# Every fourth plain residue, while wide pieces run, is summed by an accumulating DMA in place of VectorE

## The chip, the cores and the metric

The kernel runs on one core of a Trainium2 chip. The metric is the device time of one execution in microseconds (us), the median of several. TensorE's matmuls, VectorE, ScalarE and GpSimd each work through a queue of their own in the order in which the program was written; SyncE's queue issues the loads. In the rows they are PE (PEld for the loading of weights), DVE, ACT, POOL and SP.

## The reference

A trunk of two layers over 256 tokens of width 2048, all in float32. Layer 0 mixes by two groups of attention heads, layer 1 by latent attention, and each layer ends in a SwiGLU:

```python
for layer in range(DEPTH):
    ...
    x = layer_norm(DEEPNORM_ALPHA * x + y, ln_g[layer, 0], ln_b[layer, 0])
    y = swiglu(x, ffn_w_gate[layer], ffn_w_up[layer], ffn_w_down[layer])
    x = layer_norm(DEEPNORM_ALPHA * x + y, ln_g[layer, 1], ln_b[layer, 1])

def swiglu(x, w_gate, w_up, w_down):
    return (jax.nn.silu(x @ w_gate) * (x @ w_up)) @ w_down
```

w_gate and w_up are 2048 x 5632, w_down is 5632 x 2048. The change touches the two SwiGLU parts alone.

## The kernel before

**Split products.** A float32 product is made of three matmuls in TensorE's rounded float32 format. A weight w is split into a high part, w rounded, and a low part, the residue w - high; the activations lie split in the same way in XH and XL (or YH and YL). The sum is XH x high + XH x low + XL x high (`mm3`, L117 to L119). The low part is used by every second of the three matmuls, L118.

**Pieces.** All weights arrive in pieces of 256 rows. A *plain* piece is two times 512 columns (a tile of 128 x 1024): it is loaded from HBM into a raw tile by SyncE (L360), ScalarE rounds it into `wh` (L425), VectorE subtracts and writes the residue into `wl` (L427), and TensorE uses both in 12 matmuls of 512 columns, a *visit*. While a SwiGLU runs, other weights, most of w_gate and a part of w_up, go another way, which trades additions for matmuls (Strassen's scheme): these are the *wide* pieces. Their raw tile `sraw` gets sums of its own quarters from VectorE (L383 to L386), ScalarE rounds 128 x 1792 into `sh` (L389), VectorE writes the residue `sl` (L392), and TensorE uses them in 21 matmuls of 256 columns (L453 to L455). When the eighth wide piece of a chunk is done, VectorE combines four sums from PSUM, the *drain* (L483 to L489), and makes the product of gate and up (L1089, L1093); TensorE then transposes the result (L602).

**Order.** `visits` is the list of all visits, written out when the program is made; wide visits are strewn among plain ones at a rate that grows from 0.575 to 0.9 for one plain visit. `pieces` is the order in which pieces are first used. The feed keeps ahead of TensorE: after each visit that is a piece's last, its weight buffer is put back, and `feed_more` splits the next pieces (`feed_split`) for which a buffer is free, and issues loads (`feed_dma`) for which a raw tile is free. There are four raw tiles and four pairs `wh`, `wl` for plain pieces, two `sraw` and two pairs `sh`, `sl` for wide ones; while wide pieces run, the plain pieces keep to their four, which go round in turn. A wide piece's L389 and L392 are not issued with its sums but *owed*: a later split pays them (`pay`), each behind its own instruction on the same engine, and `feed_more` pays all that are older than one visit. A raw tile goes back to the list as soon as its residue has been issued; SyncE's next load into it waits on the chip until that residue is written.

`first_s` and `last_s` hold, for each layer, the positions in `pieces` of its first and last wide piece. GpSimd has small tasks in the layer norms (L978, L1006, L1007) and nothing between them in a SwiGLU.

Of the kernel before, what the change touches and what calls it, by code (L numbers as in the profile page):

```python
# [9 lines left out]
F32 = mybir.dt.float32  # L10
F32R = mybir.dt.float32r
AF = mybir.ActivationFunctionType
ALU = mybir.AluOpType
# [40 lines left out]
def trunk_kernel(ctx: ExitStack, tc: tile.TileContext, x, ab_w_in, b_f, ab_w_out,  # L54
                 rel_bias, mla_w_in, q_g, kv_g, w_uq, w_ukv, mla_w_out, w_gate, w_up,
                 w_down, ln_g, ln_b, cst, out):
    nc = tc.nc
# [67 lines left out]
    def add_chunk(name, xs, kslots, srcs, tags=None):  # L125
        subs = []
        o = 0
        for n in srcs[0]:
            subs.append((n, o))
            o += n  # L130
        c = Chunk(name, xs, kslots, subs, srcs[1], tags or ("mm",) * len(subs))
        c.n = o
        chunks[name] = c
        return c
# [28 lines left out]
    def rows(w, k0, cols):  # L163
        return [(o, n, w[k0:k0 + 256, c0:c0 + n].rearrange("(k p) c -> p k c", p=P))
                for o, n, c0 in cols]
# [3 lines left out]
    for g in range(4):  # L169
        q0, k0, v0 = ((QA, KA, VA) if g < 2 else (QB, KB, VB))  # L170
        h4 = HB4[g] % 8
        if g == 0:
            c = add_chunk("v0", "X", K16, ([260, 260], lambda h: rows(
                w0, h * 256, [(0, 520, VA + 512)])), ("mm", "att"))
        else:
            c = add_chunk(f"v{g}", "X", K16, ([512], lambda h, a=v0 + h4 * P: rows(
                w0, h * 256, [(0, 512, a)])))
        kmajor(c)
        for u in range(2):
            a = (h4 + 2 * u) * P  # L180
            c = add_chunk(f"qk{g}{u}", "X", K16, ([512], lambda h, a=a, q0=q0, k0=k0: rows(
                w0, h * 256, [(0, 256, q0 + a), (256, 256, k0 + a)])))
# [93 lines left out]
    c = add_chunk("m0", "X", K16, ([512], lambda h: rows(wi, h * 256, [(0, 512, 0)])))  # L276
    lead_begin(c)
    for i in (1, 2):
        c = add_chunk(f"m{i}", "X", K16, ([288], lambda h, i=i: rows(
            wi, h * 256, [(0, 288, 512 + 288 * (i - 1))])), ("att",) if i == 1 else None)  # L280
# [4 lines left out]
    for nm in order:  # L285
        p = int(nm[2:])
        if nm[0] == "u":
            c = add_chunk(nm, "X", [0, 1, 2, 3], ([384], lambda h, p=p: rows(
                w_uq[0], h * 256, [(0, 384, p * 384)])))
        else:  # L290
            c = add_chunk(nm, "X", [4, 5, 6, 7], ([512], lambda h, p=p: rows(
                w_ukv[0], h * 256, [(0, 512, p * 512)])))
# [6 lines left out]
    pieces = []  # L299
# [9 lines left out]
    first_s, last_s = {}, {}  # L309
# [4 lines left out]
    raw_free = [("N", feed.tile([P, HPMAX], F32, name=f"raw{i}")) for i in range(NR)]  # L314
# [5 lines left out]
    slot_of, rslot_of = {}, {}  # L320
# [20 lines left out]
    def take(free, j):  # L341
        ok = classes(j)
        for i, (k, t) in enumerate(free):
            if k in ok:
                return free.pop(i)
        return None
# [18 lines left out]
    whole = {}  # L365
    owed = []

    def pay(step):

        for o in list(owed):  # L370
            while o["fns"] and (step == "all" or o["age"] >= 1 and step == o["fns"][0][0]):
                o["fns"].pop(0)[1]()
            if not o["fns"]:
                owed.remove(o)

    def owe(key, act, dve, age=0):
        owed.append({"key": key, "age": age, "at": cur[0], "fns": [("act", act), ("dve", dve)]})

    def split_s(j):
        r = raws.pop(j)  # L380
        sh, sl = slot_of[j][1]
        v = r.rearrange("p (q c) -> p q c", c=256)
        nc.vector.tensor_tensor(v[:, 4:6], v[:, 0:1].broadcast_to([P, 2, 256]), v[:, 1:3],  # L383
                                op=ALU.subtract)
        nc.vector.tensor_tensor(v[:, 6], v[:, 1], v[:, 5], op=ALU.subtract)
        nc.vector.tensor_tensor(v[:, 7], v[:, 3], v[:, 6], op=ALU.subtract)  # L386

        def hi():
            nc.scalar.activation(sh, r[:, 256:2048], AF.Copy)  # L389

        def lo():
            nc.vector.tensor_tensor(sl, r[:, 256:2048], sh.bitcast(F32), op=ALU.subtract)  # L392
            raw_free.append(rslot_of.pop(j))
        wts[j] = (sh.rearrange("p (q c) -> p q c", c=256), sl.rearrange("p (q c) -> p q c", c=256))
        return hi, lo

    def feed_split(j, halves=False, part=None):
        if j >= len(pieces):
            return False
        c, h = pieces[j]  # L400
        n = 2 * c.n
        if part != 1:
            got = take(w_free, j) if j in raws else None
            if got is None:
                return False
            slot_of[j] = got
            if c.S:
                new = split_s(j)
                for o in owed:
                    o["age"] += 1  # L410
                pay("act")
                pay("dve")
                owe(j, *new)
                return True
            r = raws.pop(j)
            wh, wl = got[1]
            wts[j] = (wh[:, :n].rearrange("p (k c) -> p k c", k=2),
                      wl[:, :n].rearrange("p (k c) -> p k c", k=2))
            whole[j] = (r, wh, wl)
        r, wh, wl = whole[j]  # L420
        cuts = [(0, c.n), (c.n, n)] if halves or part is not None else [(0, n)]
        if part is not None:
            cuts = [cuts[part]]
        for a, b in cuts:
            nc.scalar.activation(wh[:, a:b], r[:, a:b], AF.Copy)  # L425
            pay("act")
            nc.vector.tensor_tensor(wl[:, a:b], r[:, a:b], wh[:, a:b].bitcast(F32),  # L427
                                    op=ALU.subtract)
            pay("dve")
        if part != 0:  # L430
            whole.pop(j)
            raw_free.append(rslot_of.pop(j))
        for o in owed:
            o["age"] += 1
        return True
# [7 lines left out]
    def feed_more(lim):  # L443
        fetch()
        while fs["nsp"] < min(lim, len(pieces)) and feed_split(fs["nsp"]):
            fs["nsp"] += 1
            fetch()
        if any(cur[0] - o["at"] >= 1 for o in owed):
            pay("all")
# [577 lines left out]
    def setup_ln(c3, nxt, final=False):  # L1027
# [20 lines left out]
        def split_a():  # L1048
            assert fs["nsp"] == p0 + 4
            assert feed_split(p0 + 4, part=0)  # L1050
            fs["nsp"] += 1
# [5 lines left out]
        at((c3.name, b0 + LEAD - 3, (1,)), lambda: (ln_T(0, 0), split_a(), ln_blk_act(0, 2)))  # L1057
        at((c3.name, b0 + LEAD - 2, (1,)), lambda: ln_T(0, 1))
        at((nxt.name, 1, (0,)), lambda: (ln_T(0, 2), feed_split(p0 + 4, part=1)))
        at((nxt.name, LEAD - 3, (0,)), lambda: (ln_T(1, 0), ln_blk(1, 1)))  # L1060
        at((nxt.name, LEAD - 2, (0,)), lambda: (ln_blk_act(0, 3), ln_blk(1, 2)))
# [295 lines left out]
    for i, (c, h, toks, *half) in enumerate(visits):  # L1357
# [21 lines left out]
        if last_use[c.name, h] == i:  # L1379
            j = pid[c.name, h]  # L1380
# [81 lines left out]
```

## Time and profile before

| | us |
|---|---|
| median of 3 runs | 2145.41 (2145.27 to 2146.47) |
| the profiled execution | 2146.55 |
| its span, first to last instruction | 2144.7 |
| TensorE busy | 2120.4 (99%) |
| VectorE busy | 1674.0 (78%) |
| ScalarE busy | 1061.6 (50%) |
| GpSimd busy | 94.5 (4%) |

The SwiGLU of layer 0 takes some 440 to 1140 us of the span and that of layer 1 the time from 1437 on; wide pieces run from 465 to 1050 and from 1455 to 2047. The granted clock of TensorE is 1.00 in nearly all of the span (mean 0.998), the higher of its two levels. A busy TensorE is not TensorE at its peak, since its matmuls overlap; what counts is whether it waits. In the rows "idle before <- releaser" is the time in which an engine had nothing to do ahead of an instruction, and what ended it.

### The profile page before, as it was taken

The numbers are of one execution on the slowest core, as the hardware profiler recorded it, in microseconds if no ns is written. First come the engines' busy times: TensorE is split into PE (matmuls) and PEld (weight loads), VectorE is DVE, ScalarE is ACT, GpSimd is POOL, SyncE is SP. The second block draws the span as 40 slices with busy tenths as digits, with TensorE's granted clock in tenths as the row PEclk, the third lists the DMA queues.
The fourth block names the chain that finished last, engine by engine and source line by source line (L and its number), as shares of the span: only waits on it lengthen the run. The fifth ranks groups of instructions, "written<-read, shape, count | busy, mean of one in ns | idle before, by whom it ended". The sixth has DMA issues, their size and how long they took to land.

```text
span 2144.7 us, 31708 instructions
## 1 busy us (share of the span) xinstructions
PE 2120.4 (99%) x12570; PEld 1864.7 (87%) x12570; DVE 1674.0 (78%) x2173; ACT 1061.6 (50%) x1212; POOL 94.5 (4%) x142
## 2 busy tenths in 40 slices
PE   9999999999999999999999999999999999999998
PEld 9899998788888888888888999878888888888886
DVE  5555656798888998899866676688888989889875
ACT  5444544355545555555534665445444555555551
POOL 2100000100000000000001331010000000000000
PEclk9999999999999999999999999999999999999999
DMA  8565555556555556555865533745555556555582
GB/s 287 176 204 165 172 184 199 198 174 207 195 191 190 189 190 203 187 187 184 295 193 164 176 129 137 284 139 182 188 189 192 180 190 203 187 190 199 184 293 77
DMA packets 230341, 410.41 MB, mean 191 GB/s; under 512 B 14089, under 2 KB 58161, under 8 KB 229169
## 3 DMA queue, kind: packets, MB, share of 16 engines
q1 hardware_dynamic: 230192, 408.40, 57.3%
q8 instruction: 98, 1.61, 0.3%
q14 instruction: 51, 0.41, 0.1%
HBM read 402.56 MB, written 5.78 MB: 190 GB/s over the span
## 4 chain that ended last, share of the span: by engine, by line
PE 58%; issue 35%; DVE 5%; ACT 1%; POOL 1%; DMA 0%; SPq 0%; DVEq 0%; ACTq 0%; POOLq 0%
PE mm L117 11%; PE mm L118 11%; PE mm L119 11%; PE mm L512 3%; PE mm L516 3%; PE mm L514 3%; PE tp L602 2%; PE att L118 1%; PE att L119 1%; PE att L117 1%; PE sA L454 1%; PE sB L454 1%; PE sC L454 1%; PE sC L455 1%; PE sB L453 1%
## 5 line engine op out<-in xcount | busy, mean ns | idle before, releaser
L425 ACT ACTIVATE wh<-raw 128x1024 fp32r<-128x1024 f32 (+3 forms) x403 | 417.5, 1040 | 416.2 <-PE mm L119 161.9
L427 DVE TENSOR_TENSOR wl<-raw,wh 128x1024 fp32r<-128x1024 f32 (+3 forms) x403 | 482.3, 1206 | 133.1 <-ACT wh L425 131.9
L392 DVE TENSOR_TENSOR sl<-sraw,sh 128x1792 fp32r<-128x1792 f32 x176 | 356.2, 2024 | 64.6 <-ACT sh L389 63.9
L389 ACT ACTIVATE sh<-sraw 128x1792 fp32r<-128x1792 f32 x176 | 298.9, 1698 | 145.1 <-DVE sraw L386 141.9
L117 PE MATMUL mm<-wh,XH 128*128 128x512 f32 (+3 forms) x820 | 319.9, 390 | 0.0
L118 PE MATMUL mm<-wl,XH 128*128 128x512 f32 (+3 forms) x820 | 316.8, 386 | 0.0
L119 PE MATMUL mm<-wh,XL 128*128 128x512 f32 (+3 forms) x820 | 316.3, 386 | 0.0
L117 PE MATMUL mm<-wh,YH 128*128 128x512 f32 (+1 forms) x768 | 303.9, 396 | 0.0
L118 PE MATMUL mm<-wl,YH 128*128 128x512 f32 (+1 forms) x768 | 302.9, 394 | 0.0
L119 PE MATMUL mm<-wh,YL 128*128 128x512 f32 (+1 forms) x768 | 302.4, 394 | 0.0
L119 PEld LDWEIGHTS mm<-wh,XL 128*128 128x128 f32 x820 | 153.9, 188 | 33.2
L117 PEld LDWEIGHTS mm<-wh,XH 128*128 128x128 f32 x820 | 154.4, 188 | 28.0
L118 PEld LDWEIGHTS mm<-wl,XH 128*128 128x128 f32 x820 | 154.1, 188 | 27.7
L119 PEld LDWEIGHTS mm<-wh,YL 128*128 128x128 f32 x768 | 144.1, 188 | 34.6
L117 PEld LDWEIGHTS mm<-wh,YH 128*128 128x128 f32 x768 | 144.5, 188 | 29.6
L118 PEld LDWEIGHTS mm<-wl,YH 128*128 128x128 f32 x768 | 144.2, 188 | 29.5
L383 DVE TENSOR_TENSOR sraw<-sraw 128x512 f32<-128x512 f32 x176 | 120.5, 685 | 0.0
L512 PE MATMUL mm<-XH,wh 128*128 128x256 f32 x364 | 104.3, 286 | 0.0
L514 PE MATMUL mm<-XH,wl 128*128 128x256 f32 x364 | 102.6, 282 | 0.0
L516 PE MATMUL mm<-XL,wh 128*128 128x256 f32 x364 | 102.5, 282 | 0.0
L453 PE MATMUL sA<-sh,XH 128*128 128x256 f32 x352 | 100.9, 287 | 0.0
L454 PE MATMUL sA<-sl,XH 128*128 128x256 f32 x352 | 98.8, 281 | 0.5 <-DVE sl L392 0.4
(302 smaller groups left out, 4447.6 us busy)
## 6 DMA issues: line engine op xcount, KB each, us to landing
raw<-in_ffn_w_down_dram SPq DMA_DIRECT2D x160, 512.0 KB, 5.2
sraw<-in_ffn_w_gate_dram SPq DMA_DIRECT2D x149, 512.0 KB, 3.9
raw<-in_ffn_w_up_dram SPq DMA_DIRECT2D x137, 512.0 KB, 4.7
raw<-in_ab_w_in_dram SPq DMA_DIRECT2D x80, 256.0 KB, 3.1
sraw<-in_ffn_w_up_dram SPq DMA_DIRECT2D x39, 512.0 KB, 3.9
raw<-in_ffn_w_gate_dram SPq DMA_DIRECT2D x27, 512.0 KB, 4.6
sraw<-in_ab_w_in_dram SPq DMA_DIRECT2D x48, 256.0 KB, 3.3
raw<-in_ab_w_out_dram SPq DMA_DIRECT2D x22, 512.0 KB, 3.6
```

Source lines behind the costliest of these rows:

```text
L117: nc.tensor.matmul(o, lh, rh, start=start, stop=False)
L118: nc.tensor.matmul(o, lh, rl, start=False, stop=False)
L119: nc.tensor.matmul(o, ll, rh, start=False, stop=stop)
L389: nc.scalar.activation(sh, r[:, 256:2048], AF.Copy)
L392: nc.vector.tensor_tensor(sl, r[:, 256:2048], sh.bitcast(F32), op=ALU.subtract)
L425: nc.scalar.activation(wh[:, a:b], r[:, a:b], AF.Copy)
L427: nc.vector.tensor_tensor(wl[:, a:b], r[:, a:b], wh[:, a:b].bitcast(F32), op=ALU.subtract)
L453: nc.tensor.matmul(o, h, w[0][:, q], start=first, stop=False)
L454: nc.tensor.matmul(o, h, w[1][:, q], start=False, stop=False)
L512: nc.tensor.matmul(o, wh[:, kk, a:a + P], XH[:, slot, :], start=first, stop=False)
L514: nc.tensor.matmul(o, wl[:, kk, a:a + P], XH[:, slot, :], start=False, stop=False)
L516: nc.tensor.matmul(o, wh[:, kk, a:a + P], XL[:, slot, :], start=False, stop=last)
```

## The change

`by_dma` chooses pieces of the up and down weights (`u`, `d`) whose place lies more than six pieces behind the first wide piece of their layer and ahead of the last, and of these every fourth plain one, counted over all plain pieces. For them `feed_split` issues no residue on VectorE. ScalarE rounds the raw tile into `wh` as before (now L434), then writes the negative of `wh` into `wl` (L435), and GpSimd issues a DMA (L436) that adds the raw tile to `wl`. This path pays nothing that is owed; the raw tile's next load and TensorE's matmul with `wl` wait for the DMA's completion.

```diff
--- before.py
+++ after.py
@@ -394,6 +394,18 @@
         wts[j] = (sh.rearrange("p (q c) -> p q c", c=256), sl.rearrange("p (q c) -> p q c", c=256))
         return hi, lo
 
+    nth = {}
+    for j, (c, h) in enumerate(pieces):
+        if not c.S:
+            nth[j] = len(nth)
+
+    def by_dma(j):
+
+        c, h = pieces[j]
+        y = c.name[1]
+        return (c.name[0] in "ud" and y in first_s and first_s[y] + 6 < j < last_s[y]
+                and nth[j] % 4 == 0)
+
     def feed_split(j, halves=False, part=None):
         if j >= len(pieces):
             return False
@@ -418,6 +430,15 @@
                       wl[:, :n].rearrange("p (k c) -> p k c", k=2))
             whole[j] = (r, wh, wl)
         r, wh, wl = whole[j]
+        if part is None and by_dma(j):
+            nc.scalar.activation(wh[:, :n], r[:, :n], AF.Copy)
+            nc.scalar.activation(wl[:, :n], wh[:, :n].bitcast(F32), AF.Copy, scale=-1.0)
+            nc.gpsimd.dma_start(out=wl[:, :n].bitcast(F32), in_=r[:, :n], accum_op=ALU.add)
+            whole.pop(j)
+            raw_free.append(rslot_of.pop(j))
+            for o in owed:
+                o["age"] += 1
+            return True
         cuts = [(0, c.n), (c.n, n)] if halves or part is not None else [(0, n)]
         if part is not None:
             cuts = [cuts[part]]
```

The chosen pieces all have the third pair, `wh2` and `wl2`; in layer 0 they come from the raw tile `raw1`, in layer 1 from `raw2`. 62 pieces are chosen, 31 in a layer. The rows of the built order follow; the lines of the changed kernel are 21 higher behind the inserted code (L446 for L425, L448 for L427, L505 for L484, L1105 for L1084).

ScalarE, layer 0, behind the fourth drain (`gt` is the gate tile, `sh1` the rounded wide piece), before:

```order
L1084 ACTIVATE gt221_3530<-gt221_3530 128x1024
L425 ACTIVATE wh1_96<-raw0_88 128x1024
L425 ACTIVATE wh2_98<-raw1_89 128x1024
L389 ACTIVATE sh1_104<-sraw0_92 128x1792
L425 ACTIVATE wh3_100<-raw2_90 128x1024
L389 ACTIVATE sh0_102<-sraw1_93 128x1792
```

and after:

```order
L1105 ACTIVATE gt221_3530<-gt221_3530 128x1024
L446 ACTIVATE wh1_96<-raw0_88 128x1024
L434 ACTIVATE wh2_98<-raw1_89 128x1024
L435 ACTIVATE wl2_99<-wh2_98 128x1024
L389 ACTIVATE sh1_104<-sraw0_92 128x1792
L446 ACTIVATE wh3_100<-raw2_90 128x1024
L389 ACTIVATE sh0_102<-sraw1_93 128x1792
```

One instruction stands more, between the plain piece's rounding and the wide one's. Behind the 62 copies stand a wide rounding L389 in 34 cases, the rounding of the next plain piece in 18, and the evacuation of a transpose (L113) in 10. But for one place in each layer, where such an L113 now stands ahead of an L389, the order of the other instructions is what it was.

VectorE at the same place, before:

```order
L386 TENSOR_TENSOR sraw0_92<-sraw0_92 128x256
L427 TENSOR_TENSOR wl1_97<-raw0_88,wh1_96 128x1024
L427 TENSOR_TENSOR wl2_99<-raw1_89,wh2_98 128x1024
L392 TENSOR_TENSOR sl1_105<-sraw0_92,sh1_104 128x1792
L383 TENSOR_TENSOR sraw1_93<-sraw1_93 128x512
```

and after:

```order
L386 TENSOR_TENSOR sraw0_92<-sraw0_92 128x256
L448 TENSOR_TENSOR wl1_97<-raw0_88,wh1_96 128x1024
L392 TENSOR_TENSOR sl1_105<-sraw0_92,sh1_104 128x1792
L383 TENSOR_TENSOR sraw1_93<-sraw1_93 128x512
L385 TENSOR_TENSOR sraw1_93<-sraw1_93 128x256
```

The residue of `wl2` is gone from between that of `wl1` and the wide piece's.

GpSimd, layer 0, from the first layer norm (`mv`, `X`) to the second, before:

```order
L1006 TENSOR_TENSOR X_3525<-X_3525,G_3536 128x512
L1007 TENSOR_TENSOR X_3525<-X_3525,B_3537 128x512
L978 TENSOR_TENSOR mv_3532<-mv_3532,neghalf 128x1
L1006 TENSOR_TENSOR X_3525<-X_3525,G_8990 128x512
L1007 TENSOR_TENSOR X_3525<-X_3525,B_8991 128x512
```

and after:

```order
L1027 TENSOR_TENSOR X_3525<-X_3525,G_3536 128x512
L1028 TENSOR_TENSOR X_3525<-X_3525,B_3537 128x512
L436 DMA wl_99<-raw_89 128x1024 x31
L999 TENSOR_TENSOR mv_3532<-mv_3532,neghalf 128x1
L1027 TENSOR_TENSOR X_3525<-X_3525,G_9021 128x512
```

The 31 DMAs of the layer stand between the two layer norms, one behind the other.

## Rows read from the trace of the kernel before

**Rows 1.** The page: busy us of each engine (share of the span) and instructions
```profile
PE 2120.4 (99%) x12570; PEld 1864.7 (87%) x12570; DVE 1674.0 (78%) x2173; ACT 1061.6 (50%) x1212; POOL 94.5 (4%) x142
```

**Rows 2.** Waits of TensorE: who waited for whom, us in total, times, longest
```profile
PE tp L602 <- DVE gt L1093: 2.7, 2, 1.4
PE tp L602 <- DVE gt L1089: 2.5, 3, 1.3
```

**Rows 3.** One stretch, 700 to 1055: busy us, clock, DMA share, GB/s
```profile
700.00:1055.00 355.00, 353.19 (x2120) 311.09 (x2119) 321.75 (x373) 185.10 (x156) 0.00 (x0) 1.00 0.59 197
```

**Rows 4.** Timeline, 839 to 845, SyncE's queue and VectorE: start, duration, idle before
```profile
839.38 0.37 SPq L360 DMA_DIRECT2D sraw<-in_ffn_w_gate_dram  x1
839.27 0.68 DVE L383 TENSOR_TENSOR sraw<-sraw 128x512 f32<-128x512 f32 x1
842.78 2.03 DVE L392 TENSOR_TENSOR sl<-sraw,sh 128x1792 fp32r<-128x1792 f32 x1 [0.77 <-ACT sh L389]
844.72 0.69 DVE L383 TENSOR_TENSOR sraw<-sraw 128x512 f32<-128x512 f32 x1
```

**Rows 5.** Groups by form, 440 to 1060: busy us, mean ns, idle before
```profile
L427 DVE TENSOR_TENSOR wl<-raw,wh 128x1024 fp32r<-128x1024 f32 x135 | 163.2, 1220 | 19.9 <-ACT wh L425 19.4
```

**Rows 6.** Timeline, 1033 to 1039, ScalarE, VectorE, TensorE
```profile
1033.58 1.06 ACT L425 ACTIVATE wh<-raw 128x1024 fp32r<-128x1024 f32 x1 [0.35 <-DMA raw<-in_ffn_w_up_dram]
1036.27 2.03 DVE L392 TENSOR_TENSOR sl<-sraw,sh 128x1792 fp32r<-128x1792 f32 x1
1038.35 0.39 PE L454 MATMUL sA<-sl,XH 128*128 128x256 f32 x1
```

**Rows 7.** Timeline, 817 to 822, VectorE and ScalarE
```profile
817.79 2.35 DVE L427 TENSOR_TENSOR wl<-raw,wh 128x1024 fp32r<-128x1024 f32 x2
818.47 1.69 ACT L389 ACTIVATE sh<-sraw 128x1792 fp32r<-128x1792 f32 x1
820.19 2.03 DVE L392 TENSOR_TENSOR sl<-sraw,sh 128x1792 fp32r<-128x1792 f32 x1
```

**Rows 8.** Timeline, 1509 to 1525, VectorE and TensorE
```profile
1509.68 2.02 DVE L392 TENSOR_TENSOR sl<-sraw,sh 128x1792 fp32r<-128x1792 f32 x1 [0.37 <-ACT sh L389]
1524.35 0.65 PE L602 MATMUL tp<-ident,gt 128*128 128x128 f32 x4 [1.30 <-DVE gt L1089]
```

**Rows 9.** Timeline, 852 to 862, VectorE and TensorE
```profile
852.35 0.42 DVE L484 TENSOR_TENSOR gt<-gt,sD 128x256 f32<-128x256 f32 x1 [1.29 <-ACT gt L483]
859.69 2.03 DVE L392 TENSOR_TENSOR sl<-sraw,sh 128x1792 fp32r<-128x1792 f32 x1 [0.18 <-ACT sh L389]
861.77 0.38 PE L454 MATMUL sA<-sl,XH 128*128 128x256 f32 x1
```

**Rows 10.** DMA issues, 440 to 1060: count, KB each, median us to landing
```profile
sraw<-in_ffn_w_gate_dram SPq DMA_DIRECT2D x71, 512.0 KB, 3.9
raw<-in_ffn_w_down_dram SPq DMA_DIRECT2D x68, 512.0 KB, 5.2
B<-in_ln_b_dram SPq DMA_DIRECT2D x1, 1024.0 KB, 10.6
```

**Rows 11.** Groups of GpSimd: busy us, mean ns, idle before
```profile
L978 POOL TENSOR_TENSOR mv<-mv,neghalf 128x1 f32<-128x1 f32 x8 | 7.6, 952 | 1783.0 <-DVE mv L977 1783.0
```

**Rows 12.** Timeline, first and last of 62 pieces, ScalarE and TensorE
```profile
494.49 1.06 ACT L425 ACTIVATE wh<-raw 128x1024 fp32r<-128x1024 f32 x1 [2.19 <-PE mm L119]
507.62 0.39 PE L117 MATMUL mm<-wh,XH 128*128 128x512 f32 x1
...
2042.15 1.05 ACT L425 ACTIVATE wh<-raw 128x1024 fp32r<-128x1024 f32 x1
2054.88 0.40 PE L117 MATMUL mm<-wh,XH 128*128 128x512 f32 x1
```

**Rows 13.** Timeline of SyncE's queue, first and last of the 62
```profile
500.68 0.47 SPq L360 DMA_DIRECT2D raw<-in_ffn_w_down_dram  x1
...
2047.93 1.69 SPq L360 DMA_DIRECT2D raw<-in_ffn_w_down_dram  x2
```

## The prediction

> **What bounds the kernel now.** I began with the busy shares: TensorE is busy for 2120.4 of 2144.7 us [rows 1]. Next the list of waits, for TensorE alone: what it waits for longest are tiles that VectorE makes, in the two feed-forward parts, 5.2 us in all [rows 2]. So there is little to win, and the question is what the change makes TensorE wait for. The table of stretches gives the place: while wide pieces run, TensorE is busy for 353.2 of 355 us, VectorE for 321.8, ScalarE for 185.1, GpSimd for none [rows 3]. VectorE is second, and the change takes work from it, so I looked at what VectorE's time consists of.
>
> The timeline shows it [rows 4]. A wide piece goes round a loop of two engines: VectorE makes the sums of the raw tile (L383 to L386, from 839.27), ScalarE rounds them (L389), VectorE takes the residue (L392, from 842.78), and at 844.72 the sums of the next wide piece begin: 5.45 us each. Before L392 VectorE was idle for 0.77 us, until L389 ended. A plain residue (L427, 1.22 us) lies in the time in which VectorE waits for L389 anyway. So the reader is to see two things: taking an L427 out of that gap shortens nothing, and making L389 start later lengthens the loop.
>
> **What is removed.** 62 plain residues leave VectorE, 31 in each layer: 62 x 1.22 [rows 5] = 75.6 us of VectorE's time. By the loop I count this at 0 on the path: in each place that I follow below, L392 starts as L389 ends. The bound on the other side is the 5.2 us of [rows 2], if all these waits went.
>
> **What ScalarE gets.** 62 copies of 128x1024 into wl, at the 1.06 us of the rounding L425 of the same shape [rows 6]: 65.7 us. ScalarE is half idle, but by the order each copy stands right behind the piece's own L425, and in 34 of 62 cases a wide rounding L389 stands right behind the copy. Behind the moved piece of 817.50 such an L389 starts at 818.47, without a gap, and L392 at 820.19, 0.03 us after L389 ends [rows 7]: with the copy between, L392 starts 1.06 us later. Such a delay stays in the loop until VectorE or ScalarE next waits for TensorE, and costs TensorE nothing while wide pieces are ready early. I followed it to the places where they are not:
> (a) The first drain of each layer. The moved piece at 1507.00, L389 right behind it, L392 at 1509.68, one more turn of the loop, the drain, and TensorE's transpose at 1524.35, which already waits 1.30 us for VectorE [rows 8]. I found no gap in any link: 1.06 us, all of it on the path.
> (b) 779 to 861. Moved pieces at 779.49, 797.52, 817.50 and 834.64 have an L389 right behind (the third is in [rows 7]): 4 x 1.06 = 4.24. VectorE next waits for another engine at 852.35, 1.29 us [rows 9], which absorbs that much: 2.95. The moved piece at 857.07 adds 1.06: 4.0. There L392 ends at 861.72 (859.69 and 2.03), and TensorE's matmul on its tile starts at 861.77 [rows 9]: no reserve, 4.0 us on the path.
> (c) 1011 to 1038. A moved piece at 1011.40 adds 1.06; one at 1032.17 adds 1.06 less the 0.35 us for which ScalarE waits ahead of the next rounding: 0.71. L392 ends at 1038.30 and its matmul starts at 1038.35 [rows 6]: 1.8 us.
> Together 6.9 us a layer; the second layer runs alike, so 13.7. Bounds: 0, if the delays are made good elsewhere, and 62 x 1.06 = 66 if none is.
>
> **What GpSimd and the DMA engines get.** 62 accumulating DMAs of 512 KB. The trace shows no DMA issued by GpSimd and none that adds, so their time from the end of the copy to landing, X, is bounded by neighbours. Lower: one wide load of 512 KB, 3.9 us from issue to landing [rows 10]. Upper: a load of 1,024 KB (one row of HBM spread to all partitions), 10.6 us [rows 10], since the addition has to read two tiles of 512 KB, and for the issue GpSimd's instruction on one column, 0.95 us [rows 11]: 11.6. I take what is nearest in kind, a plain load issued 0.4 us behind a wide one, 1,024 KB together, landing 5.2 us after its own issue [rows 10], 5.6 after the first; with 0.95 for the issue X = 6.6 us.
>
> Who waits for it: TensorE's second matmul of the piece, and SyncE, which may load the raw tile again only after landing. TensorE first. For all 62 pieces I took the time from the start of L425 plus 2.12 (two passes of ScalarE) to the first matmul on that buffer: 494.49 to 507.62 leaves 11.0 us in the first of the 62, 2042.15 to 2054.88 leaves 10.6 in the last [rows 12]; the middle one has 10.9. At X = 6.6 three fall short, by 1.0 us in all: that is the term. At 11.6, 53 fall short, by 79 us. SyncE likewise, to its next load of that raw tile: 500.68 leaves 4.1 us in the first and 2047.93 leaves 3.7 in the last [rows 13]; at X = 6.6 it would wait in 16 of the 62, up to 3.6 us. Behind it stand the next loads; since it mostly waits for the wide raw tile anyhow, 0.
>
> The Trainium skill, "DMA: Bandwidth & Descriptors", section "Anatomy of one DMA — SWDGE (gpsimd) path", gives about 2.0 us plus bytes over 436 GB/s for a plain DMA that GpSimd issues, an estimate of 3.2 us for 512 KB; by it the term of 1.0 would be 0. No run here shows it, and nothing in the sum hangs on it.
>
> Sharing of the 16 engines: loads keep them busy for 0.59 of the time at 197 GB/s [rows 3], 334 GB/s while busy, so 512 KB take 1.6 us. A wide load beside an accumulation may land that much later; it has 5.34 us between its issue at 839.38 and its use at 844.72 [rows 4] and needs 3.9, a reserve of 1.4. The rest, 0.2 us, for the 7 moved pieces of (b) and (c) in each layer: 14 x 0.2 = 2.8 us.
>
> **The sum.** 13.7 + 1.0 + 2.8 = 17.5 us. The profiled execution took 2146.55 us (the span of 2144.7 and 1.85 around it), the median of the runs is 2145.41; on the median this gives 2163 us, 0.8% slower. GpSimd has nothing else queued between the layer norms, so its waiting for the copies holds up nobody.
>
> **Rivals.**
> 1. Hidden: the loop makes the delays of (b) and (c) good, because with fewer residues in VectorE's queue some L392 that stand behind two L427 today start sooner. Against it: in [rows 7] the pair of L427 ends at 820.14, just as L389 does (820.16). Then (a) is left at most: 2145 to 2149.
> 2. Faster: VectorE's 75.6 us shorten the drains of [rows 2]; nearly all of the 5.2 us gone gives 2141. Against it: [rows 8], where L389 bounds what is ahead of the drain. It decides if L392 there starts sooner after its L425 than today, which the copy between them hinders.
> 3. Slow landing: X above 10.9 us, from where half of all pieces make TensorE wait. At 11.6 the price is 79 us beside 13.7 and 2.8: 2241. For it: the 10.6 us of [rows 10]; against it: 5.6 for the same bytes in two loads.
> 4. GpSimd held up by VectorE at each issue. VectorE is busy for 0.91 of these stretches [rows 3], and an issue that has to let one L392 pass waits up to 2.03 us [rows 4]: X = 8.6, where 8 pieces fall short by 11.9 us in place of 1.0: 2174. Against it: no row of these stretches shows GpSimd at work at all. The Trainium skill, "SBUF — State Buffer", section "Who interferes with whom", says that a VectorE in its two-port modes locks GpSimd out of a port pair that both use, so that such DMAs starve, but that a tensor_tensor takes only the read side; no run here shows either.
> 5. That the change doesn't do what it says is excluded by the order: 62 DMAs on GpSimd, 62 L427 fewer.
>
> **How the numbers follow.** The forecast (2150 to 2172) gets 0.48, rival 1 0.21, rival 2 0.09, rival 3 0.15, rival 4 0.07. About 0.2% (4.3 us) is what a measurement here tells from no change. Slower: 0.48 + 0.15 + 0.07 = 0.70; same 0.21; faster 0.09. The range leaves out most of rival 2 and most of rival 3: 2143 to 2215, the upper end being X = 11 (49 us of waits and the 16.5 of the other terms, so 2211).
>
> **What would show it.** Right: TensorE's waits for L392 or its drains grow by about 4 us near 822 to 861 and 2 us near 1030, the transpose of (a) waits 1 us longer, VectorE is some 75 us less busy and ScalarE 65 more, landings take 5.5 to 8 us. Wrong: landings above 10.9 us, with TensorE waiting for wl at the DMA; or no new wait of TensorE, so that the loop is less stiff than I read it. A wait of SyncE for the accumulations with late wide loads behind it would be a step that I put at 0.

## The result, and the profile after

The changed kernel takes 2164.72 us (2163.86 to 2165.81, 4 runs), the kernel before 2145.94: a ratio of 1.0088 with an interval of 1.0070 to 1.0105, 18.8 us slower. The forecast was 2163. The runs below show that the total agrees better than the working behind it does.

The page of the changed kernel (busy us of each engine, then the queue of GpSimd's DMAs with packets, MB and its share of 16 engines, then their count, KB and median us to landing):

```profile
PE 2129.8 (98%) x12570; PEld 1870.4 (86%) x12570; DVE 1603.2 (74%) x2111; ACT 1122.6 (52%) x1274; POOL 148.5 (7%) x204
...
q0 software_dynamic: 8928, 32.51, 7.8%
...
wl<-raw POOLq DMA_DIRECT2D x62, 512.0 KB, 5.2
```

VectorE has 70.8 us less to do than in [rows 1], ScalarE 61.0 more, and the span has grown from 2144.7 to 2162.9. TensorE's "busy" has grown by 9.4 us although it does the same work, which is a first hint that part of the loss is slower matmuls and not waiting. The waits of TensorE (us in total, times, longest):

```profile
PE sA L475 <- DVE sl L392: 5.7, 6, 1.7
PE tp L623 <- DVE gt L1110: 4.5, 3, 2.3
PE tp L623 <- DVE X L953: 2.7, 2, 1.5
```

Beside those of [rows 2], the kernel before had these two:

```profile
PE tp L602 <- DVE X L932: 1.0, 2, 0.8
PE sA L454 <- DVE sl L392: 0.4, 2, 0.2
```

Against them the drains L1110 (L1089 before) have grown by 2.0, the waits for X, to which the feed-forward's output is added, by 1.7, and waits for the wide residue L392 have come up, 5.7 us where there were 0.4. No wait of TensorE for an accumulating DMA is among them. The place (b) of the prediction shows the cause. The timeline of ScalarE, VectorE and TensorE there:

```profile
860.73 1.04 ACT L434 ACTIVATE wh<-raw 128x1024 fp32r<-128x1024 f32 x1
861.81 1.06 ACT L435 ACTIVATE wl<-wh 128x1024 fp32r<-128x1024 f32 x1
862.78 1.69 ACT L389 ACTIVATE sh<-sraw 128x1792 fp32r<-128x1792 f32 x1
...
864.50 2.02 DVE L392 TENSOR_TENSOR sl<-sraw,sh 128x1792 fp32r<-128x1792 f32 x1 [2.41 <-ACT sh L389]
...
866.58 0.39 PE L475 MATMUL sA<-sl,XH 128*128 128x256 f32 x1 [1.67 <-DVE sl L392]
```

The reader is to see the chain without a gap: rounding, copy, wide rounding, wide residue, matmul. VectorE sits idle for 2.41 us ahead of L392, where [rows 9] had 0.18. The same matmul as in [rows 9] starts 4.81 us later than before, and then something follows that the prediction had not counted. Stretches of 2 us there (busy time of PE, PEld, DVE, ACT, POOL, then the granted clock, DMA share, GB/s):

```profile
864.00:866.00 2.00, 0.90 (x4) 0.36 (x2) 1.50 (x1) 1.41 (x2) 0.14 (x1) 1.00 0.69 133
866.00:868.00 2.00, 1.43 (x9) 1.43 (x10) 1.93 (x5) 0.00 (x0) 0.00 (x0) 0.80 0.87 156
868.00:870.00 2.00, 2.00 (x11) 2.00 (x11) 1.33 (x3) 1.70 (x1) 0.00 (x0) 0.50 0.96 338
870.00:872.00 2.00, 2.00 (x11) 1.72 (x10) 2.00 (x2) 0.24 (x1) 0.00 (x0) 0.84 0.41 160
```

TensorE was busy for 0.90 of the 2 us from 864; from 867 on the granted clock is 0.50, the lower level (1.2 GHz), for some 3.4 us; by the starts of the same matmuls that costs 1.5. There are three such stretches in the two feed-forward parts of the changed kernel (this place, 1536 and 1874), 4.5 us together, and none in the kernel before.

Starts of the same matmuls, after less before, give the account by place; the last one starts 18.5 us later. The first drain: 1.0 us in layer 0, 2.5 in layer 1 (1.5 of them clock). 861 and its like at 1858: 3.7 and 3.9 (1.5 each clock). 1011 to 1038 and its like: 1.8 and 1.1. That is 14.0 of the 18.5 us, at the three places that were named; 1.7 more come at the waits for X, 0.8 stand there within the first 11 us, ahead of every moved piece, and the rest comes in steps of less than 0.5. At the named places the account holds what the copies and what the DMAs do; the experiments part the two.

### The profile page after: what moved, and what is told of

Read it like the earlier page. It is cut to its first block, busy times and chain, and to the rows that moved or that the text cites. A ratio compares the mean times of both kernels' runs of the same rounds, so it can differ in the third digit from the quotient of the medians.

```text
span 2162.9 us, 31890 instructions
## 1 busy us (share of the span) xinstructions
PE 2129.8 (98%) x12570; PEld 1870.4 (86%) x12570; DVE 1603.2 (74%) x2111; ACT 1122.6 (52%) x1274; POOL 148.5 (7%) x204
## 5 line engine op out<-in xcount | busy, mean ns | idle before, releaser
L446 ACT ACTIVATE wh<-raw 128x1024 fp32r<-128x1024 f32 (+4 forms) x341 | 352.1, 1036 | 338.5 <-PE mm L119 114.3
L448 DVE TENSOR_TENSOR wl<-raw,wh 128x1024 fp32r<-128x1024 f32 (+4 forms) x341 | 408.9, 1204 | 136.0 <-ACT wh L446 133.1
L392 DVE TENSOR_TENSOR sl<-sraw,sh 128x1792 fp32r<-128x1792 f32 x176 | 356.2, 2024 | 144.5 <-ACT sh L389 144.1
L389 ACT ACTIVATE sh<-sraw 128x1792 fp32r<-128x1792 f32 x176 | 298.5, 1696 | 130.0 <-DVE sraw L386 97.8
L436 POOL DMA_DIRECT2D wl<-raw x62 | 54.0, 870 | 1194.2 <-ACT wl L435 1064.7
L383 DVE TENSOR_TENSOR sraw<-sraw 128x512 f32<-128x512 f32 x176 | 120.5, 685 | 0.0
```

## The experiments

Each is compared with the kernel before on the same chip (medians of 2146.25 to 2146.38 us). The edits are to these lines of the changed kernel:

```
nc.scalar.activation(wh[:, :n], r[:, :n], AF.Copy)                                       # L434
nc.scalar.activation(wl[:, :n], wh[:, :n].bitcast(F32), AF.Copy, scale=-1.0)             # L435, the copy
nc.gpsimd.dma_start(out=wl[:, :n].bitcast(F32), in_=r[:, :n], accum_op=ALU.add)          # L436, the DMA
```

### The parts one by one

**no_residue**: L435 and L436 out.

> The 62 pieces are rounded by ScalarE as before, but nothing makes their low part: no residue, no copy, no DMA (the low part that TensorE uses is an old one). Theory (the copies on ScalarE ahead of the wide roundings cost nearly all of the 18.8 us): 2144 to 2147, as before, since VectorE's relief shortens nothing. Rival, VectorE's relief is worth something: 2140 to 2143. Rival, the new order costs by itself: 2150 or more.

Measured: 2146.17 us, ratio 0.9998 (0.9989 to 1.0007). The 62 residues are worth nothing even when nothing takes their place. In this order of the work there is nothing to win by taking them off VectorE, whatever is put in their place.

**copy_alone**: L436 out.

> The changed kernel without its accumulating DMAs: residue gone, copies on ScalarE kept (the low part is left at minus the high part). Theory (the copies carry the cost): 2159 to 2165, with TensorE waiting for L392 near 862 and 1048, for the drain near 1535, as in the changed kernel. Rival (the DMAs' share of the 16 engines and SyncE's waits for them carry it): 2146 to 2152.

Measured: 2158.65, ratio 1.0059 (1.0045 to 1.0073): 12.4 us. The waits are those of the changed kernel:

```profile
PE sA L474 <- DVE sl L392: 6.5, 7, 1.7
PE tp L622 <- DVE gt L1109: 4.5, 3, 2.3
```

**dma_alone**: L435 out.

> The changed kernel without its copies on ScalarE: residue gone, 62 accumulating DMAs kept (they add to whatever the low part's buffer held). Theory (the copies carry the cost): 2145 to 2149, the upper end being my 2.8 us for late wide loads. Rival (the DMAs carry it): 2157 to 2165.

Measured: 2162.4, ratio 1.0075 (1.0062 to 1.0088): 16.1 us. My theory falls here. Copies and DMAs both carry a large cost, and 12.4 and 16.1 make 28.5 where the change costs 18.8. The waits are others than with the copies, drains and X more than L392:

```profile
PE tp L622 <- DVE gt L1113: 4.9, 2, 2.5
PE tp L622 <- DVE X L952: 3.1, 2, 1.6
PE sA L473 <- DVE gt L505: 2.8, 2, 2.0
...
PE mm L118 <- DMA wl<-raw: 1.6, 2, 1.4
```

The last line is TensorE's wait for an accumulation itself, at the last moved piece of each layer; the lines above it are waits for VectorE.

One of the places, in the timeline of this run (GpSimd's DMA, SyncE's loads, ScalarE, VectorE):

```profile
973.82 0.87 POOL L435 DMA_DIRECT2D wl<-raw  x1 [20.42 <-DMA raw<-in_ffn_w_down_dram]
975.24 0.37 SPq L360 DMA_DIRECT2D sraw<-in_ffn_w_gate_dram  x1
975.65 1.30 SPq L360 DMA_DIRECT2D raw<-in_ffn_w_down_dram  x1
...
983.34 1.06 ACT L445 ACTIVATE wh<-raw 128x1024 fp32r<-128x1024 f32 x1 [4.23 <-DMA raw<-in_ffn_w_down_dram]
984.31 1.69 ACT L389 ACTIVATE sh<-sraw 128x1792 fp32r<-128x1792 f32 x1
...
986.02 2.03 DVE L392 TENSOR_TENSOR sl<-sraw,sh 128x1792 fp32r<-128x1792 f32 x1 [0.37 <-ACT sh L389]
```

and the same instructions in the kernel before:

```profile
972.01 0.47 SPq L360 DMA_DIRECT2D raw<-in_ffn_w_down_dram  x1
...
976.98 1.06 ACT L425 ACTIVATE wh<-raw 128x1024 fp32r<-128x1024 f32 x1 [1.49 <-DMA raw<-in_ffn_w_down_dram]
979.24 1.70 ACT L389 ACTIVATE sh<-sraw 128x1792 fp32r<-128x1792 f32 x1 [1.20 <-PE mm L119]
```

The plain load behind the accumulation lands 7.7 us after its issue in place of 4.9. ScalarE waits 4.23 us for it, and the wide rounding L389, which has nothing to do with that load, stands behind it in ScalarE's queue. From there it is the loop of the prediction. Over all pairs of the same load in both traces, the first plain load issued behind an accumulation lands 0.9 us later on average (56 pairs, at most 3.4), the first wide one 0.8 (55 pairs).

### What in the DMA costs

**dma_from_wh**: L435 out, and in L436

```diff
-in_=r[:, :n]
+in_=wh[:, :n].bitcast(F32)
```

> The run dma_alone (accumulating DMAs, no copies, no residues; 2162.4) with the DMA reading the rounded tile in place of the raw tile, so that SyncE's next load of the raw tile needn't wait for it (the low part is then something else). Theory (the loads that run beside an accumulation land later, ScalarE's plain rounding waits for them, and L389 stands behind it): 2157 to 2163. Rival (SyncE's 11 waits for the accumulations, 15.6 us in all, hold up the loads behind them): 2146 to 2152.

Measured: 2162.16, ratio 1.0073 (1.0060 to 1.0087). SyncE waits for no accumulation here, where it waited 11 times in dma_alone (15.6 us in all), and the cost is 15.8 us in place of 16.1: what holds the loads up is not SyncE's wait.

**dma_plain**: L435 out, and L436 without `accum_op=ALU.add`.

> The run dma_alone with a plain copying DMA of the same 512 KB in place of the accumulating one (the low part is then the raw piece). Theory (the 16 engines are shared by time, and an addition takes longer since it has to read both tiles): less than 16.1 us of cost but not none, 2151 to 2158, landings of 4 to 5 us. Rival (any DMA of these bytes costs the same): 2160 to 2164. Rival (only the addition collides): 2146 to 2149.

Measured: 2147.21, ratio 1.0003 (0.9995 to 1.0012). 0.8 us, which the interval does not tell from 0, and below my range: without the copies, the addition is what collides, as the second rival had it.

**dma_half**: L435 out, L436 with `:c.n` for `:n` (512 of 1024 columns).

> The run dma_alone with accumulations of half the width, 256 KB each (the other half of the low part is left as it was). Theory (sharing by bytes): the loads behind land half as much later, and part of that is hidden: 2147 to 2154. Rival (the cost lies in the issue by GpSimd or in the fixed time of a DMA, whatever its bytes): 2159 to 2164.

Measured: 2148.36, ratio 1.0007 (0.9999 to 1.0016). 2.0 us. GpSimd issues as many DMAs as in dma_alone, so it isn't the issue. The queue's row in the pages of dma_alone, of dma_half and of dma_plain:

```profile
q0 software_dynamic: 8928, 32.51, 8.3%
```

```profile
q0 software_dynamic: 8928, 16.26, 4.6%
```

```profile
q0 software_dynamic: 8928, 32.51, 3.9%
```

Share times span by 62 gives the time that the packets of one DMA take, spread over the 16 engines: 2.9 us for the accumulation of 512 KB, 1.6 for that of 256 KB, 1.35 for the plain copy of 512 KB. It is an estimate of what the engines are held for: the DMA share of a short stretch passes 1 at places (1.05 from 484 to 486 in the kernel before), so packets seem to overlap.

**dma_eighth_piece**: L435 out, and `nth[j] % 8` for `nth[j] % 4` in `by_dma`.

> The run dma_alone (2162.4) with every eighth plain piece in place of every fourth: 32 accumulating DMAs of 512 KB in place of 62, the other pieces as in the kernel before. Theory (each late load costs by itself): half of 16.1, 2151 to 2157. Rival (the losses add up along the loop and vanish when there are fewer, as half the bytes in dma_half cost 2 us): 2146 to 2150.

Measured: 2155.11, ratio 1.0040 (1.0027 to 1.0053): 8.9 us for 32 DMAs. Half the number costs half, half the size costs an eighth: the loss does not vanish with fewer accumulations, as the rival had it, and one of half the size mostly fits beside the loads. It does not come evenly with each accumulation: in the trace of this run TensorE falls behind at five places (near 703, 1009, 1700, 2006 and 2038 of the kernel before), all of them places where it falls behind in dma_alone too.

### The place of the copy

**sh_first**: the owed wide rounding ahead of the copy.

```diff
 nc.scalar.activation(wh[:, :n], r[:, :n], AF.Copy)
+pay("act")
 nc.scalar.activation(wl[:, :n], ...scale=-1.0)
 nc.gpsimd.dma_start(...)
+pay("dve")
```

> The changed kernel with one thing moved: the owed wide rounding L389 is issued ahead of the copy, not behind it; copy and DMA stay. Theory (it is the place of the copy, ahead of L389, that costs): 2146 to 2151, wide residues L392 start right after L389 as before and no wait for L392 of over 1 us is left. Rival (ScalarE's 66 us of more work cost wherever they stand, since they only delay the next rounding): 2156 to 2164. Rival (the DMAs carry it): 2160 to 2165.

Measured: 2165.53, ratio 1.0087 (1.0073 to 1.0101). Nothing gained, where I expected nearly all.

**sh_first_nodma**: the same without L436.

> The run copy_alone (copies, no DMAs, no residues: the low part is left at minus the high part; 2158.7) with the owed wide rounding L389 ahead of the copy. Theory (a copy costs where it stands ahead of L389, and the run sh_first showed nothing since the DMAs cost 16 us by themselves): 2146 to 2151. Rival (the copy costs behind L389 too, since it then delays the next plain rounding and its residue, which stands ahead of the next L392): 2155 to 2160.

Measured: 2148.70, ratio 1.0011 (1.0002 to 1.0020). So the place of the copy is what costs: 12.4 us where the change has it, 2.3 with the edit. And the 2.3 is not the price of a copy behind L389. The edit's `pay` issues a wide rounding only when it has been owed for a split, which is so in 20 of the 62 cases; in 16 the copy still stands right ahead of an L389. The order of ScalarE in this run, at (b) and at (c):

```profile
858.31 1.04 ACT L434 ACTIVATE wh<-raw 128x1024 fp32r<-128x1024 f32 x1
859.26 1.69 ACT L389 ACTIVATE sh<-sraw 128x1792 fp32r<-128x1792 f32 x1
860.85 1.04 ACT L436 ACTIVATE wl<-wh 128x1024 fp32r<-128x1024 f32 x1
...
1012.05 1.04 ACT L434 ACTIVATE wh<-raw 128x1024 fp32r<-128x1024 f32 x1
1013.12 1.06 ACT L436 ACTIVATE wl<-wh 128x1024 fp32r<-128x1024 f32 x1
1014.09 1.68 ACT L389 ACTIVATE sh<-sraw 128x1792 fp32r<-128x1792 f32 x1
```

By the starts of the matmuls TensorE loses nothing at (a) and (b), where the copies stand behind, and 1.6 and 1.2 us in the two layers at (c), where they don't: that accounts for all of the 2.3, and is a second sign that it is the place. In sh_first the accumulations take back what the edit saves. At the piece of [rows 7], the timeline of sh_first (issue of the accumulation, the next wide load, and the sums that need it):

```profile
823.91 0.87 POOL L437 DMA_DIRECT2D wl<-raw  x1 [19.05 <-ACT wl L436]
824.65 0.37 SPq L360 DMA_DIRECT2D sraw<-in_ffn_w_gate_dram  x1
...
831.20 0.69 DVE L383 TENSOR_TENSOR sraw<-sraw 128x512 f32<-128x512 f32 x1 [1.21 <-DMA sraw<-in_ffn_w_gate_dram]
```

and of the changed kernel:

```profile
823.99 0.87 POOL L436 DMA_DIRECT2D wl<-raw  x1 [20.23 <-ACT wl L435]
827.26 0.37 SPq L360 DMA_DIRECT2D sraw<-in_ffn_w_gate_dram  x1
```

With the copy ahead of L389, the wide load, which waits for L392, is issued 3.3 us behind the accumulation, and lands in 4.5 us. With L389 first it is issued 0.74 us behind it, lands in 6.5, and VectorE waits 1.21 us for it. A wide load is issued with an accumulation or within 2 us behind it in 3 of 62 cases in the changed kernel, in 19 in dma_alone, in 23 in sh_first; a plain load in 10, 25 and 35. Those loads land 2.0 to 2.5 us later than in the kernel before, in all three runs alike; what differs is how many they are. So I read it that the copy delays the loop, and so keeps its loads out of the accumulation's way, and that the two costs don't add for this reason. The counts fit; no run changes the distance alone.

**copy_plain** and **sh_first_plain**: the changed kernel and sh_first without `accum_op=ALU.add`.

> The changed kernel with a plain copying DMA in place of the accumulating one (the low part is then the raw piece). Theory (the addition's time on the DMA engines collides with loads, a plain copy's hardly does; the copies on ScalarE cost the rest): 2158 to 2161, the 2158.7 of copy_alone and the 0.8 of dma_plain. Rival (with copies there, any DMA adds what the accumulating one adds): 2163 to 2166.

> The run sh_first (the wide rounding L389 ahead of the copy, 2165.5) with a plain copying DMA in place of the accumulating one (the low part is then the raw piece). Theory (with L389 first the copy costs 2.3, and all that was left in sh_first is the addition's collision with loads): 2148 to 2152. Rival (copy behind L389 and any DMA get into each other's way): 2158 to 2165.

Measured: 2162.64, ratio 1.0076 (1.0063 to 1.0089), and 2152.49, ratio 1.0027 (1.0016 to 1.0038). The second shows that the addition's collision is 13.0 of the 19.2 us in sh_first. Both are above my numbers: with a copy there, a plain DMA costs 4 us, not 0.8. All in one table, us above the kernel before:

| | no DMA | plain DMA | accumulating DMA |
|---|---|---|---|
| no copy | -0.1 | 0.8 | 16.1 |
| sh_first's order (20 copies behind L389) | 2.3 | 6.2 | 19.2 |
| the change's order (copies ahead of L389) | 12.4 | 16.4 | 18.8 |

Loads that are about 0.4 us late on average (dma_plain and copy_plain alike, first plain load behind the DMA) cost 0.8 in the first row and 4.0 in the third. I read that as one reserve in the loop, which either the copies or the late loads use up; no run tests this reading by itself.

### Another engine for the copy

**pool_copy**: in sh_first, GpSimd makes the copy.

```diff
-nc.scalar.activation(wl[:, :n], wh[:, :n].bitcast(F32), AF.Copy, scale=-1.0)
+nc.gpsimd.tensor_scalar(wl[:, :n], wh[:, :n].bitcast(F32), -1.0, None, op0=ALU.mult)
```

> The whole computation, with GpSimd in ScalarE's place for the negated copies, its accumulating DMA behind each; ScalarE and the order of the wide roundings as in the kernel before. Theory (ScalarE is relieved, the additions collide with loads as in dma_alone and sh_first): 2158 to 2166. Rival (GpSimd's copies and VectorE slow each other down): 2168 or more, with L392 above its 2.03 us. Rival (the additions, issued some 2 us later, meet fewer loads): 2149 to 2155.

Measured: 2180.16, ratio 1.0154 (1.0140 to 1.0168): 33.9 us, the slowest. The group of GpSimd over the whole span and two of VectorE from 440 to 1060 (count, busy us, mean ns, idle before):

```profile
L436 POOL TENSOR_SCALAR wl<-wh 128x1024 fp32r<-128x1024 f32 x62 | 184.5, 2977 | 997.9 <-ACT wh L434 997.9
```

```profile
L392 DVE TENSOR_TENSOR sl<-sraw,sh 128x1792 fp32r<-128x1792 f32 x87 | 176.1, 2024 | 61.7 <-ACT sh L389 61.6
...
L383 DVE TENSOR_TENSOR sraw<-sraw 128x512 f32<-128x512 f32 x87 | 65.7, 755 | 2.6 <-DMA sraw<-in_ffn_w_gate_dram 2.6
```

GpSimd takes 2.98 us, so the accumulations land 10.6 us (median) after ScalarE starts the piece's rounding, where it was 7.8 in the changed kernel, and TensorE now waits for them:

```profile
PE mm L118 <- DMA wl<-raw: 15.7, 7, 3.8
PE tp L625 <- DVE X L955: 4.4, 2, 2.4
PE sA L477 <- DVE sl L392: 3.4, 4, 1.7
```

In five stretches of the lower clock in the feed-forward parts, 20.5 us long together, it loses about 10 us more (an estimate, half of their length). VectorE's sums are slower (L383 takes 755 ns in place of 685 on average), which can show in the waits for X and L392, half of those for the accumulations; L392 kept its 2.02 us, so the rival was right on the total and wrong on the reason. The expected 2158 to 2166 left out that the reserve until TensorE's use, 10.9 us in the middle of the 62 pieces, would not hold for an X lengthened by a collision and by the slower copy at once.

## Why the prediction came out right, and where it was wrong

**Removed work at 0**: right, by no_residue (0.1 us less, inside its interval). Rival 2 (faster) had nothing to live on, and rival 1 (hidden) would have needed the copies to be absorbed, which they were not.

**Copies, 13.7 us**: right in mechanism and place, and nearly in size: alone they cost 12.4, and the account by place has 14.0 at (a), (b) and (c). Within that the terms were off in two ways that offset each other. The loop was less stiff than I read it: at (b) the matmul's own delay in layer 0 was 2.2 us, not 4.0. And the clock, which the sum priced at nothing, added 4.5 us: after a wait TensorE ran at the lower level for some microseconds at three of the six places. Part of the 14.0 is also the DMAs' (the next steps), so that it meets 13.7 so closely is partly luck.

**Time to landing, X = 6.6, and its 1.0 us**: X was 5.6 us from the copy's end (4.8 to 10.5), and TensorE never waited for an accumulation, though the closest landed 0.5 us ahead of its use. Rival 3 needed X above 10.9 for half of the pieces and had it for none. Rival 4, GpSimd held up at each issue, is out: the issues took 0.85 to 1.09 us, in all 62 cases. The pieces in [rows 12] and [rows 13] are not the first and the last of the 62: the first moved piece is rounded at 478.98 in the kernel before and the last at 2029.22, with 10.4 and 6.6 us left. Over the right 62 the middle is 10.9 and the term 1.0 all the same.

The Trainium skill, "DMA: Bandwidth & Descriptors", section "Anatomy of one DMA — SWDGE (gpsimd) path", gave an estimate of 3.2 us for a plain DMA of these bytes that GpSimd issues. The plain ones in dma_plain landed in 2.8 us at the least and 5.0 in the median beside the loads:

```profile
DMA to landing us min/median/max: 2.8/5.0/7.0
```

The accumulating ones took 4.5 at the least, so the estimate, which says nothing of additions, doesn't hold for them.

**Sharing of the DMA engines, 2.8 us**: this is the step that failed. With the 1.0 of landing the DMAs were to cost 3.8 us; alone they cost 16.1, and beside the copies 6.4 (18.8 less 12.4). Three things were wrong in it. An accumulation takes 2.7 to 3.0 us of the 16 engines by the shares, where I took the 1.6 us of a load of that size. I looked at wide loads only, which have a reserve, and put loads behind at 0; but a plain load that lands late stops ScalarE, and the wide rounding stands behind it in ScalarE's queue, the very chain that I had followed for the copies. And I took what delays a load to be seen from bytes and reserve, not from how soon behind the accumulation the load is issued.

**SyncE's waits at 0**: right. They came (15, 22.4 us in all); without them dma_from_wh cost 15.8 us where dma_alone cost 16.1.

**The sum**: adding the terms was wrong too. 12.4 and 16.1 became 18.8, as I read it because a loop that waits for a copy sends its loads later, out of the accumulation's way. DMA terms too small by a factor of four (3.8 against 16.1) and a sum that doesn't add cancelled each other nearly; 2163 against 2164.72 is luck in that part.

What stays open: why an accumulation takes the engines twice as long as a plain copy (the trace shows the share, not the reason), whether it is the distance to the next loads that keeps the two costs from adding, and how much of the 4 us of a plain DMA beside a copy is lost reserve.

## What to carry to other kernels

The second busiest engine of a kernel need not have anything to give: take the work out without replacement first, as in no_residue, and see whether the time moves at all. What is put in the place of a hidden instruction must be costed by what stands behind it in its queue: here 62 short passes of ScalarE cost 12.4 us ahead of the loop's rounding and 2.3 with a third of them moved behind it, among them those of (a) and (b). A DMA between two tiles is not free beside loads; look at which load is issued next, and at which instruction waits for that load and what is queued behind.

## What the runs showed of the hardware

An accumulating DMA of 512 KB between two tiles took 2.7 to 3.0 us of the 16 DMA engines by the shares, a plain one 1.35 (dma_plain), and landed in 4.5 us at the least against 2.8. 62 of the first cost 16.1 us beside the loads, 62 of the second 0.8.

GpSimd's multiplication of 128x1024 took 2.98 us on average, 2.77 undisturbed, where ScalarE's pass takes 1.06. Two places of pool_copy (GpSimd and VectorE):

```profile
841.08 3.04 POOL L436 TENSOR_SCALAR wl<-wh 128x1024 fp32r<-128x1024 f32 x1 [13.99 <-ACT wh L434]
840.79 0.68 DVE L383 TENSOR_TENSOR sraw<-sraw 128x512 f32<-128x512 f32 x1
841.51 1.14 DVE L385 TENSOR_TENSOR sraw<-sraw 128x256 f32<-128x256 f32 x1
...
960.18 2.76 POOL L436 TENSOR_SCALAR wl<-wh 128x1024 fp32r<-128x1024 f32 x1 [14.54 <-ACT wh L434]
960.21 1.55 DVE L383 TENSOR_TENSOR sraw<-sraw 128x512 f32<-128x512 f32 x1
961.80 0.42 DVE L385 TENSOR_TENSOR sraw<-sraw 128x256 f32<-128x256 f32 x1
```

It is the order and the distance of the starts that part the cases. The 11 sums L383 that had started ahead of GpSimd's instruction took 0.68 us as ever; the 18 that started behind it (by up to 1.5 us), while it ran, took 0.92 to 1.55. Of the short sums L385 and L386, the 15 that started up to 0.7 us behind took 1.14 to 1.21 in place of 0.42; the 47 that started 1.3 us and more behind took 0.42, though GpSimd's instruction still ran. The residues L392 beside it took 2.02 as ever, but they had either started ahead of it (18) or 1.5 us and more behind (27), so no row has an L392 that began as early behind GpSimd as nearly all of the slowed sums did. The Trainium skill, "SBUF — State Buffer", section "Who interferes with whom", says that a VectorE instruction with two inputs in SBUF contends with a GpSimd instruction that reads SBUF. The slowed sums agree with that; the short ones that started late, beside a GpSimd instruction that still ran, show none of it.

The granted clock fell to 0.50 behind waits of 1.67, 2.31 and 1.68 us in the changed kernel, for some 3.4 us each, which adds 1.5 us to such a wait. It did not fall behind a wait of 1.71 at 529 in the same trace, nor in copy_alone behind the 2.31 at 1534, nor behind the waits of up to 1.4 us in [rows 2]. So the length of the wait alone does not decide it, and the clock's share of the loss differs from run to run. The stretch of 2 us behind the wait at 529 (columns as above):

```profile
530.00:532.00 2.00, 2.00 (x20) 2.00 (x19) 2.00 (x2) 1.97 (x3) 0.00 (x0) 1.00 0.00 0
```
